# A four-layer hybrid decoder trunk: another order of issue on each engine, from four lists put together instead of one with a second merge

## The chip, the cores and the metric

The kernel runs on one core of a Trainium2 chip. The metric is the device time of one execution in microseconds (us): the median of three runs before the change was 2625.46 us (2624.12 to 2626.32).

## What is computed

Four layers, each `x = x + gate * mixer(rmsnorm(x) * (1 + scale) + shift)`, on 1024 positions of width 1024, batch 1, all in float32. Shift, scale and gate come from `c @ ada_w[i] + ada_b[i]`. Layers 0 and 3 mix with HGRN2, layer 1 with sliding-window attention, layer 2 with a gated DeltaNet. Each mixer has one input projection, a mixing part, a SiLU gate and one output projection. The change's prediction is mostly on layer 2:

```python
def gdn_mixer(h, w_in, w_out, conv_w, a_log, dt_bias, onorm_g):
    qkv, z, a, b = jnp.split(h @ w_in, [GD_QKV, GD_QKV + GD_VW, GD_QKV + GD_VW + GD_V_HEADS], axis=-1)
    qkv = jax.nn.silu(causal_conv(qkv, conv_w))
    q, k, v = jnp.split(qkv, [GD_QKW, 2 * GD_QKW], axis=-1)
    ...
    o = gated_delta_scan(q, k, v, beta, g)
    o = rmsnorm(o, onorm_g).reshape(B, T, GD_VW).astype(h.dtype)
    return (o * jax.nn.silu(z)) @ w_out
```

In the scan each chunk solves a triangular system `(A + I) X = rhs`, takes `v_new = u - w S`, gives an output from the old state and `v_new`, and updates the state: `S = S * exp(d_last) + k^T v_new`. The next chunk needs the new S.

## The kernel before, in words

**Tiles.** Activations are kept transposed (128 channels by 512 positions, two halves). A projection is split in three float32r matmuls per 128-row step, hi by hi, lo by hi and hi by lo (`mm3`, called with lines L350, L351, L352 for its three matmuls); a group of 8 steps, 24 matmuls of 128x512, fills one PSUM bank (`proj_ps`; other names for other projections: `projw_ps`, `projt_ps`, `outp_ps`, `out_ps`). Weights come by DMA from SyncE (`w_raw`, L319), ScalarE makes the hi part (`w_hi`, L321 or L324), VectorE the lo part (`w_lo`, L322 or L325).

**Layer 2 (`gdn`).** Its work is cut in eight units u of two value heads. Unit u runs its scan while unit u+1 has its triangular inverse made and later units are projected. The pieces that the prediction names:

- *Projections*: the evacuation of q, k and v is `conv`: ScalarE copies the bank to `gd_xs` (L820) and multiplies by the last tap into `gd_tb` (L824, after which the bank is free), VectorE adds three taps (L826), ScalarE takes a tanh (L832), VectorE multiplies (L833, into `gd_q`, `gd_k`); then TensorE transposes (`qtr_ps`, `ktr_ps`, `vtr_ps`, L839), ScalarE squares and sums (L846), and VectorE goes on from the sums (`gd_ms`, L880). The evacuation of z is a tanh on ScalarE and one product on VectorE (L918, after which the bank is free).
- *The inverse* (`inverse`): 31 pairs of VectorE instructions (L973, L974) fill `gd_Tb`; it goes through DRAM (L977 out, L983 back), ScalarE puts it in `gd_Tc` (L984), VectorE transposes that to `gd_Uc` (L986), and TensorE makes the rest in four rounds of small matmuls (`z_ps`, L1002 the first).
- *The scan* (`scan`), eight chunks a unit, each a chain from engine to engine: TensorE `ks_ps` (L1070, L1071, from the state and k, q); VectorE `gd_y` (L1076, for two heads); TensorE `w_ps` (L1081); ScalarE `gd_ws` (L1082); TensorE `S_ps` (L1086); VectorE `gd_S` (L1092), which the next chunk's `ks_ps` needs. Beside it ScalarE makes `gd_wg` (L1096) and TensorE the output (`w_ps`, L1097).

**What sets the order.** The program is first recorded by functions that weave such streams together. At its end `in_order` takes, for each engine, the recorded instructions and issues them in an order read from a table of numbers, `ORDER`: byte n of an engine's table means that the n-th instruction of those still left comes next (values from 255 up are spelled in three bytes). Each engine carries out its instructions in that order, and waits at one whose operands aren't there. Buffers, instructions and dependences are set before that, so the table moves instructions and nothing else, but for ScalarE's table loads, which are put in afterwards where its functions change.

```python
    for e, table in ORDER.items():
        left, places, last = rest[getattr(mybir.EngineType, e)], iter(zlib.decompress(base64.b85decode(table))), None
        for n in places:
            i = left.pop(n if n < 255 else next(places) + 256 * next(places))
            if last is not None:
                how = mybir.DependencyInfo(mybir.DependencyClass.NoSync, mybir.DependencyReason.DATA)
                tc.add_manual_dep(i, last, how, reason="order")
            last = i.name
```

Of the kernel before, what the change touches and what calls it, by code (L numbers as in the profile page):

```python
# [22 lines left out]
P = 128  # L23
T = 1024
D = 1024
# [31 lines left out]
        "iwx`sRaG)%n;9&`wg^-}vk$8Bfgq(0bLMh`yeg$%91-I{rUNP*(qh<haKcQxkV{%berc<`?^bC8mnktaaK)n6P-wjm0si<P%K!qk2Da%1?*4"
        "An?NWr!m2{}31KUZv=7zYm#0n7FkwWAJKJv<FU$*rR1Y$l&LkV(=fdH7&3R{-D?1%xkBgAe>EF{iV4cVksXahUemcK-DwyTEBfhHV|>b`*@h"
        "(v;AK47(7bq^Z2-|N-)iDKPJsYQoESY#w(6+4}`T+J!$L+1B)nMJTXniy^e24!WWepY@31A3StZI=YOPX^Q9V_^0$P(4b0^)G#ZEDhtQ2F_<"
        "cG=TpmAx$(I#m}#<uC}FZVC$letO2R2s1gZPXtdy2f<fwWt`WzVQp@badQg3y@7f$P=`;y-guJk)K>1Kutp?M$-Gq(~`{%lK>+t9r0A$p%`S"  # L60
        "-s9@MWRu3*lw@+(u9j@0qPsleHEZg&Sr=je={Q!-a4XNnf4%j&|X{h1^B_q@$(<Z@>MvIf;P1dtrWF{eFP1_<eW}?l}|OdmyJD@81uLu)r6$"
# [1733 lines left out]
```

## Time and profile before

| | |
|---|---|
| median of 3 runs | 2625.46 us |
| the profiled execution | 2630.06 us |
| its span, first to last instruction | 2628.4 us |
| TensorE busy in the span | 2542.7 us (97%) |
| VectorE, ScalarE busy | 2014.9 us (77%), 1328.7 us (51%) |
| mean granted TensorE clock | 0.988 of full |

The times of an instruction are from this one execution. A row of the timeline has the start, the duration, the engine and line, the operation, the output and inputs, the shapes, how many in a row, and in brackets how long the engine was idle before it and whose end it waited for. A row of the waits has a waiting instruction, the one that released it, the total in us, how often, and the longest. In a table of windows each engine has its busy us with the number of its instructions; PEclk is the clock granted to TensorE.

By time the span falls in a start (0 to about 60 us), layer 0 (to about 490), layer 1 (to about 1090), layer 2 (to about 1990) and layer 3.

### The profile page before, as it was taken

To read this page: it belongs to the slowest core of one execution; us is meant where nothing else is said; L and a number is where in the kernel's file an instruction comes from. 1 tells how busy PE (TensorE), PEld (TensorE's weight loads), DVE (VectorE), ACT (ScalarE), POOL (GpSimd) and SP (SyncE) were. 2 spreads that over 40 slices of the span, in tenths; PEclk is the share of its full clock that TensorE was granted. 3 is DMA by queue.
4 is the path that set the end of the run, shared out by engine and by line. 5 is a ranking of instruction groups with operands and counts; after the bars stand their busy time and mean duration, and the time that the engine had idled before them with its cause. 6 is when DMAs were issued, how large, how long until landed. Compare 5 with 4: busy or idle time off the path is not lost.

```text
span 2628.4 us, 50793 instructions
## 1 busy us (share of the span) xinstructions
PE 2542.7 (97%) x18271; PEld 2058.0 (78%) x18271; DVE 2014.9 (77%) x5663; ACT 1328.7 (51%) x3480; POOL 164.7 (6%) x382
## 2 busy tenths in 40 slices
PE   7999999999999999999999999999999999999999
PEld 4777887788988877787777788778788877788877
DVE  5585789886787868678889989888776846468775
ACT  4444344543465656455566666565644534344452
POOL 0001000001000000100011101100222000000000
PEclk8999999999999999999999999999999999999999
DMA  7333444644233343444344344333576412122443
GB/s 262 99 112 106 129 128 122 192 126 141 69 97 97 112 138 102 133 110 111 86 111 115 90 124 114 88 85 90 164 239 199 133 37 84 51 85 66 139 146 117
DMA packets 393618, 312.07 MB, mean 119 GB/s; under 512 B 74979, under 2 KB 320150, under 8 KB 393366
## 3 DMA queue, kind: packets, MB, share of 16 engines
q1 hardware_dynamic: 380822, 267.92, 34.5%
q0 software_dynamic: 12544, 40.90, 4.9%
q8 instruction: 144, 2.36, 0.4%
q14 instruction: 108, 0.88, 0.1%
HBM read 247.84 MB, written 60.88 MB: 117 GB/s over the span
## 4 chain that ended last, share of the span: by engine, by line
PE 80%; DVE 7%; DMA 6%; issue 4%; ACT 3%; SPq 0%; POOL 0%; DVEq 0%; ACTq 0%; POOLq 0%
PE proj_ps L350 12%; PE proj_ps L351 12%; PE proj_ps L352 12%; PE outp_ps L350 4%; PE outp_ps L351 4%; PE outp_ps L352 4%; PE projw_ps L352 2%; PE projw_ps L351 2%; PE projw_ps L350 2%; DMA ada_w<-in_ada_w_dram 2%; PE projt_ps L350 2%; PE projt_ps L351 2%; PE projt_ps L352 2%; PE lev_ps L1253 1%; PE pv_ps L1653 1%
## 5 line engine op out<-in xcount | busy, mean ns | idle before, releaser
L350 PE MATMUL proj_ps<-hhi,w_hi 128*128 128x512 f32 x1664 | 677.0, 407 | 16.4 <-ACT gd_tb L824 9.9
L352 PE MATMUL proj_ps<-hhi,w_lo 128*128 128x512 f32 x1664 | 673.4, 405 | 0.0
L351 PE MATMUL proj_ps<-hlo,w_hi 128*128 128x512 f32 x1664 | 672.1, 404 | 0.0
L350 PEld LDWEIGHTS proj_ps<-hhi,w_hi 128*128 128x128 f32 x1664 | 315.2, 190 | 80.2 <-ACT gd_tb L824 15.6
L352 PEld LDWEIGHTS proj_ps<-hhi,w_lo 128*128 128x128 f32 x1664 | 315.1, 189 | 58.2 <-issue 1.6
L351 PEld LDWEIGHTS proj_ps<-hlo,w_hi 128*128 128x128 f32 x1664 | 315.4, 190 | 56.7 <-issue 1.4
L321 ACT CAST w_hi<-w_raw 128x512 fp32r<-128x512 f32 x356 | 216.5, 612 | 266.2 <-PE proj_ps L351 150.9
L322 DVE TENSOR_TENSOR w_lo<-w_raw,w_hi 128x512 fp32r<-128x512 f32 x356 | 238.7, 675 | 129.6 <-ACT w_hi L321 124.0
L350 PE MATMUL outp_ps<-o_hi,w_hi 128*128 128x512 f32 x576 | 228.4, 398 | 1.6 <-ACT o_hi L1458 1.0
L351 PE MATMUL outp_ps<-o_lo,w_hi 128*128 128x512 f32 x576 | 229.5, 399 | 0.1
L352 PE MATMUL outp_ps<-o_hi,w_lo 128*128 128x512 f32 x576 | 228.8, 398 | 0.1
L324 ACT ACTIVATE w_hi<-w_raw,par 128x512 fp32r<-128x512 f32 (+1 forms) x136 | 94.5, 697 | 142.4 <-PE outp_ps L351 84.8
L826 DVE SCALAR_TENSOR_TENSOR gd_tb<-gd_xs,taps,gd_tb 128x512 f32<-128x512 f32 x192 | 146.0, 760 | 13.2 <-ACT gd_tb L824 12.4
L576 DVE SCALAR_TENSOR_TENSOR ada_acc<-ada_w,par,ada_acc 128x512 f32<-128x512 f32 x154 | 115.2, 748 | 35.1 <-DMA ada_w<-in_ada_w_dram 34.4
L350 PEld LDWEIGHTS outp_ps<-o_hi,w_hi 128*128 128x128 f32 x576 | 108.7, 189 | 25.0 <-issue 2.5
L325 DVE SCALAR_TENSOR_TENSOR w_lo<-w_raw,par,w_hi 128x512 fp32r<-128x512 f32 (+1 forms) x136 | 97.4, 718 | 39.9 <-ACT w_hi L324 39.5
L351 PEld LDWEIGHTS outp_ps<-o_lo,w_hi 128*128 128x128 f32 x576 | 108.9, 189 | 23.1 <-DVE o_lo L1459 1.5
L352 PEld LDWEIGHTS outp_ps<-o_hi,w_lo 128*128 128x128 f32 x576 | 108.9, 189 | 22.4 <-issue 0.9
L1450 POOL DMA_DIRECT2D o_in<-od x72 | 38.8, 539 | 1183.2 <-DVE sw_zs L1593 321.0
L350 PE MATMUL projw_ps<-w_hi,hhi 128*128 128x512 f32 x256 | 101.6, 402 | 2.4 <-DVE hg_q L1169 2.3
L351 PE MATMUL projw_ps<-w_lo,hhi 128*128 128x512 f32 x256 | 102.5, 402 | 0.0
L352 PE MATMUL projw_ps<-w_hi,hlo 128*128 128x512 f32 x256 | 102.4, 402 | 0.0
(431 smaller groups left out, 5386.3 us busy)
## 6 DMA issues: line engine op xcount, KB each, us to landing
ada_w<-in_ada_w_dram SPq DMA_DIRECT2D x160, 256.0 KB, 2.8
w_raw<-in_hg_in_w_dram SPq DMA_DIRECT2D x148, 256.0 KB, 2.9
w_raw<-in_gd_in_w_dram SPq DMA_DIRECT2D x128, 256.0 KB, 3.0
o_in<-od POOLq DMA_DIRECT2D x72, 256.0 KB, 3.6
x<-xd SPq DMA_DIRECT2D x64, 256.0 KB, 4.8
w_raw<-in_gd_out_w_dram SPq DMA_DIRECT2D x64, 256.0 KB, 3.2
xd<-x POOLq DMA_DIRECT2D x48, 256.0 KB, 2.7
w_raw<-in_sw_in_w_dram SPq DMA_DIRECT2D x44, 256.0 KB, 3.0
```

The source lines that it names most:

```text
L321: nc.scalar.copy(hi, raw)
L322: nc.vector.tensor_tensor(lo, raw, hi.bitcast(F32), ALU.subtract)
L324: nc.scalar.activation(hi, raw, AF.Copy, scale=scale)
L325: nc.vector.scalar_tensor_tensor(lo, raw, scale, hi.bitcast(F32), ALU.mult, ALU.subtract)
L350: mm(out, a[0], b[0], start=start, stop=False)
L351: mm(out, a[0], b[1], start=False, stop=False)
L352: mm(out, a[1], b[0], start=False, stop=stop)
L576: self.step = self.nc.vector.scalar_tensor_tensor(acc, w, c, acc, ALU.mult, ALU.add)
L826: last = nc.vector.scalar_tensor_tensor(y, xs[:, j:j + HT], w(j), y, ALU.mult, ALU.add)
L1253: return nc.tensor.matmul(pl[gs, n, c * 48:(c + 1) * 48], k[:, c * P + g * 32:c * P + (g + 1) * 32], x[:, 4 * c + g, :], start=True, stop= ...
L1450: nc.gpsimd.dma_start(t, od[(k0 + k) * P:(k0 + k + 1) * P, sl])
L1653: self.tied([lambda b=b, a=a: nc.tensor.matmul(po[a * 64:(a + 1) * 64], vg[:, n + 1 - nkb + b, :], p4s[b][:, :, a, :], start=b == nkb - 1, ...
```

## The change

`ORDER`'s five tables are replaced; no other line is touched. The new table is put together from four lists, one per layer, each made with assumed times of its own for handing a result from engine to engine, and TensorE's list isn't merged a second time afterwards. The tables tell a reader nothing; one line of TensorE's:

```diff
-        "c-rlo>2nmv6~N!FW>>qqZwawlohu2nI*?!`ap*z<gySF)?1(!7a~KHm2jU2m3J`<{kV>4wI1q4Ta8+W5xSVoTlFzB6Dqr#~Uy}SM`INk)dv>"
...
+        "c-rk+>u*%Y6+gSa`?Rr*4Xp7CWBj%kY}Q^dwy_Cs0>p%XAq7$zNT97Ms3L`wsDxlbfHZxC&_IE<snjM)TSaLiwe*p+A1YN<KU9_4Z~a?(9y9"
...
```

Every engine has the same instructions as before, except that ScalarE has 6 table loads instead of 8. Nearly all moves are short, within a layer. The new table text is two lines longer, so each line number after it is 2 higher in the changed kernel: L1083 there is L1081 here.

**TensorE at the end of a unit's scan.** In the first unit of layer 2, the seventh chunk and the first matmuls of the eighth. `ks_ps`, `w_ps` and `S_ps` are the scan's, `proj_ps` a projection's. Before:

```order
L1070 MATMUL ks_ps_14825<-gd_S_14741,gd_k_12988 128x256
L1071 MATMUL ks_ps_14825<-gd_S_14741,gd_q_13049 128x256
L1081 MATMUL w_ps_14824<-gd_y_14843,gd_uq_13096 128x128 x2
L1086 MATMUL S_ps_14861<-gd_ws_14850,gd_kt_13030 128x256
L1097 MATMUL w_ps_14824<-gd_wg_14849,gd_uq_13096 128x128 x2
L1070 MATMUL ks_ps_14946<-gd_S_14863,gd_k_12988 128x256
L1071 MATMUL ks_ps_14946<-gd_S_14863,gd_q_13049 128x256
L350 MATMUL proj_ps_14813<-hhi_11748,w_hi_14802 128x512
```

The same chunk in the changed kernel, from its first `w_ps` to its `S_ps`:

```order
L1083 MATMUL w_ps_14824<-gd_y_14843,gd_uq_13096 128x128
L353 MATMUL proj_ps_14679<-hlo_12498,w_hi_14597 128x512
L354 MATMUL proj_ps_14679<-hhi_12497,w_lo_14598 128x512
L352 MATMUL proj_ps_14679<-hhi_12497,w_hi_14597 128x512
L353 MATMUL proj_ps_14679<-hlo_12498,w_hi_14597 128x512
L354 MATMUL proj_ps_14679<-hhi_12497,w_lo_14598 128x512
L1083 MATMUL w_ps_14824<-gd_y_14843,gd_uq_13096 128x128
L352 MATMUL proj_ps_14679<-hhi_12497,w_hi_14597 128x512
L353 MATMUL proj_ps_14679<-hlo_12498,w_hi_14597 128x512
L354 MATMUL proj_ps_14679<-hhi_12497,w_lo_14598 128x512
L1088 MATMUL S_ps_14861<-gd_ws_14850,gd_kt_13030 128x256
```

The chain stood bare, one scan matmul behind the other; now three to five projection matmuls stand between a scan matmul and the one that needs its result. The projection group `proj_ps_14679` stood ahead of these chunks before.

**VectorE at the start of layer 2's first inverse rounds.** `gd_q` is the conv's end, which TensorE's transposes wait for, L918 frees a projection's bank, `ada_acc` is a step of layer 3's modulation that waits for a DMA. Before:

```order
L322 TENSOR_TENSOR w_lo_14298<-w_raw_14296,w_hi_14297 128x512
L826 SCALAR_TENSOR_TENSOR gd_tb_13982<-gd_xs_13980,taps_472,gd_tb_13982 128x512
L576 SCALAR_TENSOR_TENSOR ada_acc_14060<-ada_w_14352,par_102,ada_acc_14060 128x512
L833 SCALAR_TENSOR_TENSOR gd_q_13979<-gd_tb_13983,gd_tb_13982 128x512
L322 TENSOR_TENSOR w_lo_14304<-w_raw_14302,w_hi_14303 128x512
L880 TENSOR_SCALAR gd_ms_13647<-gd_ms_13647 128x16
L298 TENSOR_SCALAR rs_y_14002<-gd_ms_13647 128x16
L918 SCALAR_TENSOR_TENSOR gd_tb_14123<-gd_tb_14123,proj_ps_14052 128x512
```

In the changed kernel:

```order
L324 TENSOR_TENSOR w_lo_14298<-w_raw_14296,w_hi_14297 128x512
L828 SCALAR_TENSOR_TENSOR gd_tb_13982<-gd_xs_13980,taps_472,gd_tb_13982 128x512
L835 SCALAR_TENSOR_TENSOR gd_q_13979<-gd_tb_13983,gd_tb_13982 128x512
L988 STREAM_TRANSPOSE gd_Uc_13629<-gd_Tc_13619 128x512
L947 TENSOR_TENSOR gd_tmp_14093<-gd_tmp_14093,gd_cmask_12433 128x512
L1006 COPY gd_Z_12445<-z_ps_13682 32x16x32
L882 TENSOR_SCALAR gd_ms_13647<-gd_ms_13647 128x16
L920 SCALAR_TENSOR_TENSOR gd_tb_14123<-gd_tb_14123,proj_ps_14052 128x512
```

The `ada_acc` step and the second `w_lo` no longer stand ahead of `gd_q` and L918, and the transpose of `gd_Tc` and the evacuation of the first `z_ps` round now stand ahead of L918.

**TensorE at the same place.** Before, the transposes are followed by a projection:

```order
L352 MATMUL proj_ps_14139<-hhi_12497,w_lo_14135 128x512
L839 MATMUL qtr_ps_13991<-ident_86,gd_q_13979 128x128 x4
L350 MATMUL proj_ps_14216<-hhi_11748,w_hi_14205 128x512
L351 MATMUL proj_ps_14216<-hlo_11749,w_hi_14205 128x512
L352 MATMUL proj_ps_14216<-hhi_11748,w_lo_14206 128x512
```

In the changed kernel they are followed by the first round of the inverse:

```order
L354 MATMUL proj_ps_14139<-hhi_12497,w_lo_14135 128x512
L841 MATMUL qtr_ps_13991<-ident_86,gd_q_13979 128x128 x4
L1004 MATMUL z_ps_13681<-gd_Tc_13619,gd_uq_13096 32x32
L1004 MATMUL z_ps_13682<-gd_Tc_13619,gd_uq_13096 32x32
L1004 MATMUL z_ps_13681<-gd_Tc_13619,gd_uq_13096 32x32
```

The round needs `gd_Tc`; eleven matmuls of `proj_ps_14216` stood ahead of it before and none does now.

More of the change, by code (lines that the diff above doesn't have):

```diff
@@ L57 @@
[L57 to L61, printed above, removed]
@@ new lines @@
+        "mOoxQtv7u;5;{Ykrb?!7Z}XU;iu=A1JJAPf<LzH#_}csr~iY}&MDW@d(q6AZUe60xBMk<Zs7mLSYN(@WC?dR3pUqbG3}Qe)}TrLd$A;U5fFh"
+        "#{~XjoL%)Gx0$PxY9=!q$%~))%8;gU0q$U3OZpWbifK|hc;-17HEd$(9{GOSOz#^XoLp;m|lg8@Csaj`KG3(D@~<Iea3(LMOX-ohCtU_Z(-3"
+        "Qe7I~`7eI5f)EKfLPuC*oI!S*s{Ah3x+$Z5+mZwtq*U(T_gW(W(HODOkbhg%lJlz2oL!jGVwqW<a0zuc8EM)m@-XmH7jw6iQL<0Zn>xCmn)x"
+        "#5o%_fELhvAPQD5S+_7GP=$pKsgdR{6w&*Z7|yC>ZA7EST^9VxhP&d<|ZLbLY5-1^tZia=0j+m-etQP?EeDfEJG|g4IRp^73l7pGFxD7x=#7"
+        "F?4i1>?~L-*IOE!mA~V}^_I{c0<2Y4C8Li-ar;<eA;Bu#K+1yb69~H2@*UEZTQykJV(`v^SC@2UQj1VFT}n|4k;&L^69}0C4t;qDB1p1$JW7"
@@ new lines @@
+        "<SLS5)b#3Lv`wFU1fU3o)ow1-k{lgrz1%OqPg1V+^=3*{^xSKi}c!sR$MWMUvYYHS+T1aZfM$Pt2V48FrXxkg%Lf|jCC>j6YdgsZ&eR$8o<7"
+        "3vvnC(+=L*vaIg5JX7;aW*k`5)lj5hXWSBlM*?OK?FOA32hRlDEVc|QAD(QDTOd%2|=0|tqA*lO-&<$i?y}2Kr>frB+831T4D(PehA>LEf(n"
+        "?hX9I*$G0s6&+Y3L;6IO;1}b2jKduv(+J0zWkl>KKRMjD3wF-*vOuQ($0!fzHaP}8tM`Pnd&TBMgW0j3qXDkRoOC=DMk7|tp*Ml()N4m85l!"
+        "8wO1nAiX1onPR07nT6Drof!0B@aoXl>P6Ay8aB*n=qSjNRBfNe$Ls-!HDJP9WTy=U-G$&LG}Igc3xY0<>h$&Ck!9FZRNoJ+NEfZP@~F6W)d!"
+        "@RnKWt#{zy&4X~@O?ZlK-*_DX@H7H%;5uA`0|>Ll`|#d-@DnNjtWEF%{?zL`Kk%x4hj8!SJvczUKM63a-#mrT<=qH?ci_7`K2P<zrEj<%(<^"
@@ new lines @@
+        "+ra2|n<)ZD$fyK{H$%o&4w5~0hx5M0o1*ZUVPTp&N|-FM-KZi`uX0x6~G^zp|unh!suGLho-9f*0jbm`L7t5*ZbfA8L|yLWfNPIUYXJcfWjA"
+        "+Wp=af)!7|4;dvQ@ic34Zg(SF@Kfej(#g_fz6w#G>!1QQzF9om+^Py$`#!ka!S*6?_R##g*)&)xXtC0CqX3b%ZMAdZrwszK=8Zg5QWm=hmZ3"
+        "g3FiS$qtL>0aPltE^!DxBUqRfwDYbaI$k&^t1lY&<w`Hhs<C|WEtCueypFe)-_|@Yio3?v<7!lB`OA~iZ5TA_&;SyN0>mkA0m-5gSD?=N%K|"
+        "@8;7!Uyc41nI=-fT82#tl@l37bsr*dfc+RTbt|qx(61`gH0PB*n2G7#JWsrKhI{Mn*=&2^vfdr23V?cLSl#DuBE|`Wa&Y<Z?L?uFv4pPvLhy"
+        "XA_MX&ysOp>}Svdnw>pz<VYbsegl#F5%?uqe4iL5oM*~usYAItdGh4hvuAa~-y*o6gJcSAo|55>y|M9m2K9mh%};*~_wU26C?*B#AP-}@HqI"
@@ new lines @@
+        "{x@MnY@k2<A+@>(!>tULn4;Bn52S}Be^!=R1MP~U5j0WfUFwg4HNoipHlV*)k+2bK;2Y(QXXPH_ZAWdy1{T}5IlK~)-}$`mo9sPQ<(?no|BO"
+        "vL7<3vN{LI7$&ZjI<VJU>cN3256wk#>Q7P&}wkoQ`=*PoFQ~y*#kl^s>9wB-I@~SG&fLl=Oh_RfxBH6?2^weP)xG`NCaG{C`>p9Z8){GkXeQ"
+        "o^cZ_1vF>hdsgZTMa^=cy26Pc*`0efb+D^gVLF5<o4GmFDamb4=+opolM#&ncXiwG^vf$c=Q9?0eKP>}o8bw%SVNFrOvXLvMYMJDs5DRJ^h("
+        "n0MD-Qz<^kmX+994#LIoo5Ql;SqwhL2L>%Y>pJOrS_rpJ`Ivq{+=LbJDmLon)$BQBy4H(gX?W56W<z?Exh%1h*|eI3}27oG|dh=MiT-yby@O"
+        "cWm*T7Z+D-ItrUpt&0~g8JK6h#-O(gtul;gzlTm)v_l1lU{$d=WJE#I607H<3MZaQLzTlzh_+QGEBk^R_J~Au@FNlj9qvqf2Wg2#Zd8#>0*V"
@@ new lines @@
+        "ldG)EjLpIRy2J_7Sg{ike2QkrWP{a0nHzC>D9*;%KxAy7%DGMR*hGKS+Ff&+<9TnSRbpTArp-PBLj@XY049pq0sElfG3q*E_>WRab88ZDjp7"
+        "?yPU`w$dMI<>7x^WBduEVOhTM8F}KgM)N8N2zCrK%%1i_LbQOS$d9dss8VHVE+QQv6QX"),
+    "Activation": (
+        "c-oCtiE`sM3<WQVI<5O~?AXp`cW2uE|M&F)pd6>2=@fP>h9bd-hl41JK)KJnC$c2cG!4~T*s?sP$rHsG3;Ypn83oemuCu2kWLnG^Yl-#Xy~}"
+        "c<U<{^I0$J8nP;?H@ECeD)j)nOB=Ju1LZL_Ni)qUBO*x+1S;9S~y-%384vTPXmbe4U`<RJ{cQX8zza~-*8a%xD<Hil?&BazW}jFmDxC+sjC9"
+        "by_)1pK-l5|5X<esm=2()vc9#>}vNpzp$*7!h5SWvsrG$&K9dTo}@i>+x*OQ$T-121G?m6B&=GmULU65U@gcAkRey-LUCamJE9b;w1^Y&dGw"
+        "JV7Imy)!1597W)NW4pbf=XY65KBj%NSL>a{yl)UWJrr1+A;Fy!pR%5M@?>J02XqqNtp&*Z<;1l?z1V#XC$0K;G_nk**ga8kF1f0+FVKA3V#)"
+        "h$m^BL<fZ~?(nxE$grSl$w1gn1@-&wN9z)dQFkRSHKKBjI)}%Qtx`mO1ebhF*e^>Kb<Sec~Qatom-kJE4Bt(w=?yILYC}eFtN?0O13ImB_}i"
+        ")_cpIi`4hTo+qK?q(K$q4~YH)pA`Gv^Jz?XNreWCI}%gf!z$XA*_)=ayj%`DZiW<JU6UPWpiQZOcSXtt#&m?OXsS3ZrfJ9A@@w^CBWvNfs2k"
+        "36rcK<9Szt1z#1Z-EhqYQXmgW?^5O!})n@$Wde#A#zM=2a>(WprmYHGZul{~<<wIB9TviE$bg39Gme(LD`5A|TX5Ig-!qV@62Sg{TS1m@DP1"
+        "u*{&<IUJ)I#;j?N&ZPcLS3IaM1Ldc(@fKpP2)(*J>}vwZTlK%o@X_1ngadQ?7vZ{BrqP?!Q+;7gd#W$z88IqRzc>uwh0^uC3F8~Ik6C5Nb&@"
+        "UeNeQg_R%7Zl08e)Ofz5+GGUmPAM<=Bg|ai2c~M|M7RK=xJ)xCKhQ9?J^pM%JBBj5cl}>mGzhzm5;$YBNPG@`>YAl)<>k86QhdR;s?{s~Z13"
+        "=40@HGrSfh0i#lnrzL6WVBC7+0hj)bzz%93cc~Sr$=2kPQ+}RaO=i%9X?rFlIU5GN=r>t$?tz6V=GkX|Bd`UGI0I3qC3{I7G6BCwc3>ZQDv`"
+        "&liUjTXn0sh3bB9>HXbz5>(ggco~BR=kN|eLGt`moI~hIB9)w8Y#elpl#3(Mlslv<xO>lN91{qRCSh;>T)y1O+%4;JrUdL6aj2T@_1@lYw}C"
+        "!BKKx@9ss>sGn?OR<+^&!V8)X7bFE9lsk$gatQq!KOxi{UvB5n*EaX@ybBly=ftTZb!KuvDt8@|0VvfIE_j5a|uhK;^KdtvPrnizpXsQJkmW"
+        "w~9TG|130a7-TU1L`_J7j@G%eP46JLE~?P<|l7QJsihm$%Wn||Fn@o8Iy}kD<0oLxDD{&=EI^g8?K~((Vt9}jOp>9J74l-&a#P_GyTytAVZ%"
+        "0Luw3iE~V1YxHN}TQNdfjWn-b0Hnmb%0&q%!l^VgbC?zfh5|HBCKtq%}px`?rNcp8!>Wm8RAtfvrulGu7x$0-n<pGDQ3%#^lQeTa>T){19+v"
+        "Y>4E?*liw{gP-hq3bRkbg8>&B4O6;X>^&Ii;ILBH3xLWWHJ;KTAjSz2Tygj`d`9eMlRQ^<OPiT5mWWrJ>XHM}ziX`d2huNq?3Uy1~h!10y;i"
+        "Zn&hQ;!?#87d77-E_U!s!*#}rT^la0iz-_7_4?*o=7SG`Ua#{n`5UImNwN"),
@@ new lines @@
+    "SP": (
+        "c-o~@=}yBi40h67O_z0pu0w;3a*Rs|@s|fd976E^Z-MQkEiFSJ;U9_P<CD(-{6tbp5CU)HFCT_FWsukiFRe8wB$K?zkJzG!7J%xgV>$ZzL?m"
+        "=zEf_Ol-a!FF9jYRWx`B%PEF?2vOyVgnZTq)lWqq(Z+BDub{)CN4dSuqera3*oxZ;$A5b!HySvInKe1d0qf!DWp_!t?B9o)zwQU6Z&;aY5(Q"
+        "`DTCZT}S5091w`vrH*XHCKwGmd;J5D-`Iuu9aK#tt>h|P|v6Vd0Cc=#R68H)x2J6<*ItKVIMj)E6UjE0)up|ah}hSmdoMD_<TyY_Z7E*@;1>"
+        "^h_d7|P|MJh^c>Vqln6qnB_}IAkDTRKMiYUv5<$XmD836Nx0YaRM#bVodhU<beOi<k%-XjLfl<0*<P0PwxywX|fqpQKXn-<p`L8InQ7saIKt"
+        "hQAeLg9QE|OFfA})-<R6?i$DpDMz8JTyZ=eTWJnb^Ki&iCWG@f(AHw0?f#Lg{9E)mQm{h<223%zONIL`64Iy!re^;E%win~-cI!O{ILiG?m8"
+        "elR4d=r{1|W8ZXt%-Qzx+T7gU-T$<%R1dLpk6YO%Ge8(G"),
```

149 lines of the change are left out of this document (56 added, 93 removed).

## The prediction

> **What bounds the kernel now.** First the page's head: the span and what each engine did of it.
>
> ```profile
> span 2628.4 us, 50793 instructions
> PE 2542.7 (97%) x18271; PEld 2058.0 (78%) x18271; DVE 2014.9 (77%) x5663; ACT 1328.7 (51%) x3480; POOL 164.7 (6%) x382
> ```
>
> TensorE (PE) is the bound. No instruction is added or taken from it, so the change can only give back what isn't useful work: about 2628.4 - 2542.7 = 85.7 us of idleness, and matmuls that run at a lowered clock. Next the windows, one per layer, to see where that lies.
>
> ```profile
> 0.00:60.00 60.00, 44.96 (x159) 25.34 (x160) 35.41 (x110) 25.09 (x44) 1.11 (x8) 0.82 0.79 287
> 60.00:490.00 430.00, 419.66 (x3728) 335.33 (x3727) 320.69 (x1032) 186.08 (x475) 11.01 (x45) 1.00 0.41 123
> 490.00:1090.00 600.00, 589.86 (x3753) 490.21 (x3753) 477.59 (x1239) 319.35 (x747) 35.77 (x74) 0.99 0.37 115
> 1090.00:1990.00 900.00, 858.16 (x5774) 698.48 (x5773) 755.92 (x2055) 526.06 (x1588) 95.84 (x216) 0.99 0.43 120
> 1990.00:2629.00 639.00, 630.03 (x4862) 508.68 (x4860) 425.24 (x1231) 272.12 (x630) 20.95 (x39) 1.00 0.33 102
> ```
>
> TensorE is idle for 15.0 us in the start, 10.3 in layer 0, 10.1 in layer 1, 41.8 in layer 2 and 9.0 in layer 3. Half of it is in layer 2, where VectorE works 755.92 of 900 us as well. So third, TensorE's waits in layer 2.
>
> ```profile
> PE proj_ps L350 <- ACT gd_tb L824: 9.9, 10, 1.6
> PE proj_ps L350 <- DVE gd_tb L918: 4.8, 2, 2.4
> PE w_ps L1081 <- DVE gd_y L1076: 3.9, 5, 0.9
> PE S_ps L1086 <- ACT gd_ws L1082: 3.0, 6, 0.6
> PE w_ps L1097 <- ACT gd_wg L1096: 2.6, 6, 0.6
> PE w_ps L1081 <- ACT gd_ws L1082: 2.5, 5, 0.5
> PE ks_ps L1070 <- DVE gd_S L1092: 2.3, 3, 1.2
> PE qtr_ps L839 <- DVE gd_q L833: 1.5, 1, 1.5
> ```
>
> Five of the rows are links of one chain, the scan: 3.9 + 3.0 + 2.6 + 2.5 + 2.3 = 14.3 us in 25 waits. They aren't spread over the 64 chunks. They stand in clusters where TensorE has run out of projection matmuls to put between the links, as the timeline of one unit's end shows.
>
> ```profile
> 1277.48 0.40 PE L352 MATMUL proj_ps<-hhi,w_lo 128*128 128x512 f32 x1
> 1277.71 0.39 PE L350 MATMUL proj_ps<-hhi,w_hi 128*128 128x512 f32 x1
> 1277.94 0.38 PE L1081 MATMUL w_ps<-gd_y,gd_uq 128*128 128x128 f32 x2
> 1278.08 0.48 PE L351 MATMUL proj_ps<-hlo,w_hi 128*128 128x512 f32 x1
> 1278.39 0.40 PE L352 MATMUL proj_ps<-hhi,w_lo 128*128 128x512 f32 x1
> 1278.78 0.70 PE L1086 MATMUL S_ps<-gd_ws,gd_kt 128*128 128x256 f32 x2
> ...
> 1281.06 0.59 PE L1071 MATMUL ks_ps<-gd_S,gd_q 128*128 128x256 f32 x2
> 1282.58 0.49 PE L1081 MATMUL w_ps<-gd_y,gd_uq 128*128 128x128 f32 x2 [0.92 <-DVE gd_y L1076]
> 1283.53 0.49 PE L1081 MATMUL w_ps<-gd_y,gd_uq 128*128 128x128 f32 x2 [0.46 <-ACT gd_ws L1082]
> 1284.47 1.22 PE L1086 MATMUL S_ps<-gd_ws,gd_kt 128*128 128x256 f32 x2 [0.46 <-ACT gd_ws L1082]
> ...
> 1289.36 0.63 PE L351 MATMUL proj_ps<-hlo,w_hi 128*128 128x512 f32 x1
> ```
>
> A link over ScalarE takes 0.84 us from start to start when ScalarE is free (1277.94 to 1278.78, with two projection matmuls between), and as much or more with nothing between (0.94 from 1283.53 to 1284.47): the matmuls between cost no time, and without them TensorE stands.
>
> **The change, part by part.** *The scan's links.* I counted in the two orders how much TensorE work stands between a matmul whose result is handed out and the one that waits for it, over the five kinds of link above: 30 of 274 links have at most one 128x512 matmul between in the order before, 5 of 274 in the new one. Most others now have three or more. A matmul pair of the scan lasts 0.14 us to the next start (1277.94 to 1278.08) and a projection matmul 0.23 (1277.48 to 1277.71), so three of them and the pair make at least 0.14 + 3 x 0.23 = 0.83 us, the 0.84 of a free ScalarE link. So 25 of 30 bare links get cover, and I let the same share of their waits go: 25/30 x 14.3 = 11.9 us saved. What is late next at these places is the projection, whose matmuls now go between the links instead of ahead of them: its bank must be free about a group later, which is harmless while L824 and L918 keep their places.
>
> *The clock behind the bare links.* The windows around three such clusters have the granted clock in the column ahead of the DMA share.
>
> ```profile
> 1285.00:1290.00 5.00, 4.48 (x13) 3.48 (x12) 4.11 (x13) 3.41 (x16) 0.00 (x0) 0.50 0.22 56
> 1290.00:1295.00 5.00, 5.00 (x23) 4.16 (x23) 3.02 (x10) 1.96 (x6) 0.10 (x1) 0.87 0.01 2
> 1660.00:1665.00 5.00, 5.00 (x18) 4.08 (x18) 3.90 (x15) 2.72 (x14) 0.00 (x0) 0.66 0.20 52
> 1880.00:1885.00 5.00, 4.14 (x15) 3.44 (x16) 1.98 (x5) 2.19 (x8) 1.06 (x2) 0.68 0.18 67
> 1890.00:1895.00 5.00, 5.00 (x23) 4.17 (x21) 3.25 (x7) 2.63 (x9) 2.32 (x5) 0.80 0.58 193
> ```
>
> Busy time times the missing share of the clock is what a dip costs: 4.48 x 0.50 + 5.00 x 0.13 + 5.00 x 0.34 = 4.6 us for the first two clusters, 4.14 x 0.32 + 5.00 x 0.20 = 2.3 for the third. In the new order the first two clusters are covered throughout; the third, in the last unit, keeps some of the bare links, so I take half of it: 4.6 + 1.2, say 6 us saved.
>
> [...]
>
> *Links that get shorter.* To cover the bare links the new order spreads the same matmuls over more places: nine links over `gd_y` have about three matmuls between, and none of that kind had in the old order. VectorE can be busy when such a link asks for it: with nothing between the link took 1.52 us from start to start (1281.06 to 1282.58). With the pair's own time and three matmuls about 1.1 us of it is covered. Bounds: 0 to 0.4 us for each of nine, 0 to 4 us; I take the middle, 2 us lost.
>
> *VectorE's order at 1217 us.* Two steps move out of the way of `gd_q` and of L918.
>
> ```profile
> 1216.28 0.74 DVE L826 SCALAR_TENSOR_TENSOR gd_tb<-gd_xs,taps,gd_tb 128x512 f32<-128x512 f32 x1
> 1217.92 0.75 DVE L576 SCALAR_TENSOR_TENSOR ada_acc<-ada_w,par,ada_acc 128x512 f32<-128x512 f32 x1 [0.90 <-DMA ada_w<-in_ada_w_dram]
> 1218.59 0.68 DVE L833 SCALAR_TENSOR_TENSOR gd_q<-gd_tb 128x512 f32<-128x512 f32 x1
> ```
>
> The step that waits for its DMA for 0.90 us goes behind `gd_q`, which can start 1.6 us sooner (1218.59 against 1216.28 + 0.74). But TensorE meets the inverse's first round next, and that needs `gd_Tc`.
>
> ```profile
> 1212.65 0.18 DVE L974 TENSOR_TENSOR gd_Tb<-gd_Tb,gd_tmp 128x16 f32<-128x16 f32 x1
> ...
> 1222.62 0.67 ACT L984 COPY gd_Tc<-gd_tmp 128x512 f32<-128x512 f32 x1 [0.48 <-DMA gd_tmp<-tblk]
> ```
>
> From the last L974 to the end of L984 are 1223.29 - 1212.83 = 10.5 us through DRAM. In the new order three VectorE steps of about 0.7 us (a `w_lo`, the other half's `gd_q`, an `ada_acc`) stand behind the last L974 instead of ahead of it, so `gd_Tc` may come 1 to 3 us earlier, still after the transposes. The 1.5 us wait for `gd_q` and most of the 2.4 us wait for L918 become one wait for `gd_Tc` of about the same length. Between a gain of 3 and a loss of 3 I take 0.
>
> *Everything else.* The largest wait of layer 2, 9.9 us for L824, keeps about a whole group of 24 matmuls between in both orders: 0, at most half of it gained or as much lost. The start (15.0 us) has the same DMA order and nearly the same TensorE order: 0. Layers 0, 1 and 3 have 10.3, 10.1 and 9.0 us of idleness, in short single waits; there the links change both ways: 0, between 5 gained and 5 lost. The two table loads that go were on ScalarE, which is idle half the time: 0 to 2 us gained, taken as 0.
>
> The sum is 11.9 + 6 - 2 = 15.9, say 16 us less. Against the profiled execution, 2630.06 us (its span and 1.7 us around it), that is 2614.1. That execution lies 4.6 us above the median of the runs, so the forecast for a median is 2625.5 - 16 = **2609.5 us**.
>
> **The rivals.**
>
> *No gain.* A projection matmul covers one link only. Those now put into the bare clusters are gone from where they stood, and the projections run later against the scan, so their banks may be asked for sooner than L824 frees them: about 30 groups in the layer losing half a microsecond each is 15 us, and all is given back. For it speaks that L824's wait is the largest already, and that VectorE works 84% of the layer. Against it, the count of bare links falls without many others getting under three matmuls. Time: **2625.5**.
>
> *Slower: the inverse's round waits for `gd_Tc`.* TensorE's first `z_ps` round stands right behind the transposes, with nothing between, in the unit shown; in four of the eight units 0.5 to 1.1 us less work stands ahead of it than before, by my count of the orders. If VectorE doesn't end the L973/L974 run earlier, TensorE stands until the trip of 10.5 us is over, and L918, now behind the transpose of `gd_Tc`, keeps the projection's bank too. At 2 us a unit, 8 x 2 = 16, the gain is gone; at 3.1 us a unit the kernel is 25 us above the forecast: **2634.5**. Against it, the three VectorE steps above stand behind the run now. No row shows what L973 and L974 do in the new mix.
>
> *More.* The list for layer 2 may relieve L824, L918 and `gd_q` too: half of 9.9 + 4.8 + 1.5 is 8 us, and half of layer 0's idleness 5 more: **2596.5**. Only the one place at 1217 us speaks for it.
>
> [...]
>
> **How the numbers follow.** Forecast 0.50, no gain 0.18, slower 0.14, more 0.10, the clock stays 0.08. The likeliest gives 2609.5. Its own range, with the bounds above (2 either way for the short links, 3 at 1217 us, 5 for L824, 5 for the other layers, not all on one side), is 2600 to 2618. The range that should hold 8 in 10 reaches from the better rival to past no gain, 2594 to 2630, and leaves out the slower one. A measurement of this kernel can tell about 0.2%, 5.3 us, from no change. Faster by more than that are the forecast, more and the clock: 0.50 + 0.10 + 0.08 = 0.68; within it no gain, 0.18; slower 0.14.
>
> **What would show it.** In the changed profile the five scan rows of TensorE's waits in layer 2 should sum to 3 to 5 us instead of 14.3, TensorE's idleness from 1090 to 1990 us should fall from 41.8 to about 30, and the windows behind the first and fifth units' scan ends should have a clock near 1.00. The waits for L824 should stay near 10 us. The prediction is wrong if the scan rows fall but other rows of that view rise by as much (then the first rival; the slower one if they are `z_ps` on `gd_Tc`), or if the span's idleness moves into another layer.

## The result and the profile after

The changed kernel took 2607.2 us (median of 4 runs, 2605.29 to 2609.54), the kernel before 2625.89 beside it (4 runs, 2624.12 to 2626.53): 18.7 us less by the medians. The ratio of the two kernels, which the later runs are compared by, is 0.9917 with a 95% interval of 0.9900 to 0.9933, which would be 21.8 us (17.6 to 26.3). Its profiled execution took 2606.59 us, with a span of 2604.9. Line numbers are 2 higher now.

The page's head, and the windows of layer 0 and layer 2 (columns as before: PE, PEld, DVE, ACT, POOL busy, clock, DMA share, GB/s):

```profile
span 2604.9 us, 50803 instructions
PE 2535.7 (97%) x18271; PEld 2054.6 (79%) x18271; DVE 2015.9 (77%) x5663; ACT 1325.8 (51%) x3478; POOL 159.4 (6%) x382
```

```profile
60.00:490.00 430.00, 421.99 (x3768) 337.19 (x3767) 322.06 (x1036) 185.54 (x477) 12.11 (x48) 1.00 0.41 124
1090.00:1990.00 900.00, 872.11 (x5858) 708.38 (x5858) 767.65 (x2076) 535.10 (x1599) 97.19 (x228) 0.99 0.46 125
```

The span is 23.5 us shorter. TensorE's idleness falls from 85.7 to 2604.9 - 2535.7 = 69.2 us, by 16.5, and its busy time by 7.0 us, for the same instructions. In the window of layer 2 it is 900 - 872.11 = 27.9 instead of 41.8 us. But layer 2 begins and ends earlier now: the same TensorE work lies between 1086 and 1968 us, where TensorE is busy for 852.25 of 882 us, so 29.8 us idle, 12.0 less than before, and about 30 was forecast. In layer 0 the idleness is 8.0 instead of 10.3. TensorE's waits from 1086 to 1968 us:

```profile
PE z_ps L1021 <- DVE gd_uq L1016: 3.7, 5, 1.1
PE w_ps L1083 <- DVE gd_y L1078: 3.5, 4, 1.5
PE proj_ps L352 <- ACT gd_tb L826: 3.3, 4, 1.3
PE z_ps L1004 <- ACT gd_Tc L986: 3.0, 3, 1.5
PE proj_ps L352 <- DVE gd_tb L920: 1.9, 1, 1.9
...
PE w_ps L1099 <- ACT gd_wg L1098: 1.3, 2, 0.8
...
PE S_ps L1088 <- ACT gd_ws L1084: 1.1, 2, 0.5
...
PE w_ps L1083 <- ACT gd_ws L1084: 0.4, 1, 0.4
...
PE ks_ps L1072 <- DVE gd_S L1094: 0.3, 2, 0.2
```

The five scan rows sum to 3.5 + 1.3 + 1.1 + 0.4 + 0.3 = 6.6 us instead of 14.3, where 3 to 5 were forecast. The wait for a projection's bank (L826, L824 before) fell from 9.9 to 3.3, where it was forecast to stay near 10, and the wait for `gd_Tc` rose from 0.6 to 3.0 us. The end of the first unit's scan, bare before, on the timeline:

```profile
1274.01 0.38 PE L1083 MATMUL w_ps<-gd_y,gd_uq 128*128 128x128 f32 x2
1274.14 0.48 PE L353 MATMUL proj_ps<-hlo,w_hi 128*128 128x512 f32 x1
...
1275.38 0.38 PE L1083 MATMUL w_ps<-gd_y,gd_uq 128*128 128x128 f32 x2
...
1276.30 0.62 PE L1088 MATMUL S_ps<-gd_ws,gd_kt 128*128 128x256 f32 x2
```

The same three matmuls stood at 1282.58, 1283.53 and 1284.47 before, with 0.92, 0.46 and 0.46 us of idleness ahead of them; now there is none, and the clock is 1.00 from 1270 to 1290 us. But the place at 1217 us has a dip of the clock that is longer than before. First its waits on the timeline, then the windows:

```profile
1215.18 0.66 PE L841 MATMUL qtr_ps<-ident,gd_q 128*128 128x128 f32 x4 [0.73 <-DVE gd_q L835]
1217.35 1.20 PE L1004 MATMUL z_ps<-gd_Tc,gd_uq 32*32 32x32 f32 x64 [1.51 <-ACT gd_Tc L986]
1219.49 0.18 PE L1012 MATMUL z_ps<-gd_Uc,gd_Z 32*32 32x32 f32 x1 [0.94 <-DVE gd_Z L1006]
```

```profile
1215.00:1220.00 5.00, 2.37 (x117) 2.05 (x119) 2.70 (x6) 4.04 (x15) 2.46 (x4) 1.00 0.92 253
1220.00:1225.00 5.00, 5.00 (x100) 4.00 (x93) 4.91 (x12) 2.82 (x8) 1.63 (x3) 0.51 0.31 112
1225.00:1230.00 5.00, 5.00 (x36) 3.65 (x34) 2.96 (x13) 1.20 (x2) 0.00 (x0) 0.50 0.35 105
```

Busy time times the missing share of the clock is 5.00 x 0.49 + 5.00 x 0.50 = 5.0 us here. Summed like this over the 5-us windows from 60 us on, the clock costs 14.6 us in this profile and 16.1 in that of before; in layer 2 alone 8.4 and 10.5.

### The profile page after: what moved, and what is told of

The parts are those of the page before. It is cut to its first block, busy times and chain, and to the rows that moved or that the text cites. A ratio compares the mean times of both kernels' runs of the same rounds, so it can differ in the third digit from the quotient of the medians.

```text
span 2604.9 us, 50803 instructions
## 1 busy us (share of the span) xinstructions
PE 2535.7 (97%) x18271; PEld 2054.6 (79%) x18271; DVE 2015.9 (77%) x5663; ACT 1325.8 (51%) x3478; POOL 159.4 (6%) x382
## 4 chain that ended last, share of the span: by engine, by line
PE 76%; DVE 9%; DMA 7%; issue 4%; ACT 2%; SPq 1%; POOL 0%; DVEq 0%; POOLq 0%; ACTq 0%
PE proj_ps L352 11%; PE proj_ps L353 11%; PE proj_ps L354 11%; PE outp_ps L352 4%; PE outp_ps L353 4%; PE outp_ps L354 4%; PE projw_ps L353 2%; PE projw_ps L354 2%; PE projw_ps L352 2%; DMA ada_w<-in_ada_w_dram 2%; PE projt_ps L353 2%; PE projt_ps L354 2%; PE projt_ps L352 2%; PE lev_ps L1255 1%; DVE gd_tb L828 1%
## 5 line engine op out<-in xcount | busy, mean ns | idle before, releaser
L828 DVE SCALAR_TENSOR_TENSOR gd_tb<-gd_xs,taps,gd_tb 128x512 f32<-128x512 f32 x192 | 145.7, 759 | 11.9 <-ACT gd_tb L826 8.8
```

The source lines that it names most:

```text
L828: last = nc.vector.scalar_tensor_tensor(y, xs[:, j:j + HT], w(j), y, ALU.mult, ALU.add)
```

## The experiments

Where two orders are joined, they are cut at places at which both had issued the same instructions on each engine. All comparisons are with the kernel before on the same chip.

**Layer 2's list alone.**

```diff
 start, layers 0 and 1: the order before
-layer 2: the order before
+layer 2: the changed kernel's order
 layer 3: the order before
```

> The new order in layer 2 alone; the start and layers 0, 1 and 3 keep the order before. Theory (the gain is layer 2's: scan links with cover, projection banks freed sooner, clock behind the scans' ends): by the times of the same instructions in the two profiles layer 2 gives 18.7 of the 23.5 us, so 17 to 19 us below the kernel before, a ratio near 0.993. The prediction's own sum put 16 us there. Rival (the gain is spread over the four lists, or the layers help each other): less than 10 us, a ratio over 0.996.

Measured: 0.9945 (0.9929 to 0.9961), 14.4 us less. The five scan rows sum to 6.5 us, the wait for L826 is 3.3 and that for `gd_Tc` 3.0, the same as in the changed kernel to 0.2 us. So most of the gain is layer 2's. The 14.4 us (10.2 to 18.7 by the interval) lie below the 17 to 19 of the theory, which the interval doesn't exclude, and above the rival's 10.

**The other lists alone.**

```diff
-start, layers 0 and 1: the order before
+start, layers 0 and 1: the changed kernel's order
 layer 2: the order before
-layer 3: the order before
+layer 3: the changed kernel's order
```

> The new order in the start and layers 0, 1 and 3; layer 2 keeps the order before. Theory: the delays of the two profiles give 2.1 us in the start and layer 0, 1.5 in layer 1 and 1.7 in layer 3, so 4 to 6 us below the kernel before, a ratio near 0.998, and layer 2's waits as before (five scan rows near 14 us). The prediction had 0 for these layers, between 5 gained and 5 lost. Rival (spread gain): 10 us or more.

Measured: 0.9982 (0.9973 to 0.9992), 4.7 us less. The waits in layer 2 are those of before (9.9 for L826; the scan rows 3.7 + 3.0 + 2.5 + 2.4 + 2.0). The two parts make 14.4 + 4.7 = 19.1 us. The whole, by its ratio as well, gave 21.8, and 20.5 and 22.6 us in its two repetitions below. With intervals of about 4 us either way the parts add up to the whole; that the lists help or hinder each other isn't seen.

**Cover taken away again.** In the changed kernel the projection matmuls in the links at seven units' scan ends go ahead of them. For the first unit:

```diff
+L354 MATMUL proj_ps_14679<-hhi_12497,w_lo_14598 128x512
 L1083 MATMUL w_ps_14824<-gd_y_14843,gd_uq_13096 128x128
-L353 MATMUL proj_ps_14679<-hlo_12498,w_hi_14597 128x512
...
 L1083 MATMUL w_ps_14824<-gd_y_14843,gd_uq_13096 128x128
-L352 MATMUL proj_ps_14679<-hhi_12497,w_hi_14597 128x512
...
 L1088 MATMUL S_ps_14861<-gd_ws_14850,gd_kt_13030 128x256
```

> The changed kernel with the links at seven units' scan ends laid bare again: TensorE's projection matmuls that stand in the seventh chunk's links (in units 1, 2, 5 and 6 also in the last links of the sixth) go ahead of these links in one piece; nothing else moves. Theory (cover is worth the idleness and the clock): a bare end stood idle for 0.61 + 0.92 + 0.46 + 0.46 + 0.52 = 3.0 us in the profile before and cost 2.9 us of clock. Four long ends and three of one chunk: 16 to 20 us of idleness and 11 us or more of clock, 25 to 32 us slower than the changed kernel, with windows under 0.90 of the clock behind at least the four long ends. [...] Rival (covering links is worth nothing, the time comes from elsewhere): under 5 us.

Measured: 1.0045 (1.0031 to 1.0060) of the kernel before, where the changed kernel has 0.9917: 0.0128 x 2626 = 34 us slower than the changed kernel, slower even than the kernel before. TensorE's waits in layer 2, the scan rows first, and five windows at or behind bare ends (the first unit's, and those of units 1, 3, 5 and 6):

```profile
PE w_ps L1083 <- ACT gd_ws L1084: 5.1, 5, 3.1
PE w_ps L1083 <- DVE gd_y L1078: 4.9, 8, 1.1
PE S_ps L1088 <- ACT gd_ws L1084: 4.3, 9, 0.5
PE w_ps L1099 <- ACT gd_wg L1098: 4.2, 8, 0.8
...
PE proj_ps L352 <- ACT gd_tb L826: 3.3, 4, 1.4
...
PE ks_ps L1072 <- DVE gd_S L1094: 2.0, 4, 0.9
```

```profile
1280.00:1285.00 5.00, 5.00 (x25) 4.00 (x23) 5.00 (x16) 4.31 (x18) 0.11 (x1) 1.00 0.40 110
...
1370.00:1375.00 5.00, 3.79 (x12) 3.12 (x13) 3.34 (x12) 3.01 (x13) 0.00 (x0) 0.67 0.39 106
...
1565.00:1570.00 5.00, 2.45 (x6) 1.68 (x6) 3.46 (x9) 3.13 (x12) 0.00 (x0) 0.62 0.03 3
...
1755.00:1760.00 5.00, 3.97 (x14) 3.12 (x15) 3.30 (x13) 3.71 (x15) 0.00 (x0) 0.74 0.31 87
...
1845.00:1850.00 5.00, 3.89 (x11) 3.05 (x12) 3.10 (x12) 1.85 (x8) 0.00 (x0) 0.61 0.15 54
```

The scan rows sum to 20.5 us, 13.9 more than in the changed kernel. Over the whole span (2636.8 us, TensorE busy for 2548.0) the idleness is 88.8 us, 19.6 more than in the changed kernel, and the busy time 12.3 us more: together the 31.9 us by which the spans differ. Of the 12.3 us, the windows put 20.9 - 14.6 = 6.3 down to the clock; the other 6 are taken up below. Three of the four long bare ends have a dip behind them, where the theory had all four: behind unit 2's the clock stays at 1.00. Of the three ends that are bare for one chunk, the first unit's and unit 4's leave it at 1.00 too; unit 3's has a dip, with a single wait of 3.08 us for a `gd_ws` that ScalarE makes late, behind work on transposes. The clock's 6.3 us are fewer than the 11 of the theory, and the loss is a little above its 25 to 32 us, with 6 us of busy time that it hadn't counted. The runs say the same of the clock: its mean over ten of them is 0.9867, against 0.990 for the changed kernel. So cover is worth both idleness and clock, as the theory had it, and the rival doesn't hold. The wait for L826 stayed at 3.3 us: it does not hang on this cover.

**The place at 1217 us put back.** TensorE has projection matmuls ahead of the first round again, VectorE the step that frees their bank ahead of the transpose, ScalarE its half ahead of `gd_Tc`. VectorE's part:

```diff
 L835 SCALAR_TENSOR_TENSOR gd_q_13979<-gd_tb_13983,gd_tb_13982 128x512
+L882 TENSOR_SCALAR gd_ms_13647<-gd_ms_13647 128x16
+L920 SCALAR_TENSOR_TENSOR gd_tb_14123<-gd_tb_14123,proj_ps_14052 128x512
 L988 STREAM_TRANSPOSE gd_Uc_13629<-gd_Tc_13619 128x512
 L947 TENSOR_TENSOR gd_tmp_14093<-gd_tmp_14093,gd_cmask_12433 128x512
 L1006 COPY gd_Z_12445<-z_ps_13682 32x16x32
-L882 TENSOR_SCALAR gd_ms_13647<-gd_ms_13647 128x16
-L920 SCALAR_TENSOR_TENSOR gd_tb_14123<-gd_tb_14123,proj_ps_14052 128x512
```

> The changed kernel with one place put back as it was before: at 1215 us VectorE and ScalarE again do the two evacuations of z ahead of the first inverse's gd_Tc and gd_Uc, and TensorE again has 11 projection matmuls ahead of the first z_ps round and 6 behind it (17 fewer at later places of the same unit). Theory (the new dip of the clock at 1220 to 1230 us comes from the stretch of idleness and 32x32 matmuls behind each other): idleness at the place stays within 1 us, the dip shrinks from 5 us to the 1 to 2 us it cost before, 3 to 4 us faster than the changed kernel, about 2603.5. Rival (the dip hangs on the idleness alone, which stays): no change, within 1 us.

Measured: 0.9910 (0.9894 to 0.9926), which can't be told from the changed kernel's 0.9917; nor can the 3 to 4 us of the theory be told from nothing at these intervals. The waits at the place and the windows:

```profile
1215.42 0.66 PE L841 MATMUL qtr_ps<-ident,gd_q 128*128 128x128 f32 x4 [0.74 <-DVE gd_q L835]
1218.52 0.50 PE L352 MATMUL proj_ps<-hhi,w_hi 128*128 128x512 f32 x1 [2.44 <-DVE gd_tb L920]
```

```profile
1220.00:1225.00 5.00, 5.00 (x169) 3.88 (x170) 2.12 (x4) 2.37 (x6) 2.89 (x5) 1.00 0.44 160
1225.00:1230.00 5.00, 5.00 (x78) 3.78 (x69) 4.54 (x14) 3.06 (x7) 0.00 (x0) 1.00 0.27 70
```

The idleness is the same 3.2 us, in two waits instead of three with small matmuls between, and in this profile the dip is gone: 5 us of clock are back. A second profile of the same kernel, from the comparison on one chip below, has a dip there again, a shorter one:

```profile
1215.00:1220.00 5.00, 2.56 (x7) 1.99 (x7) 3.05 (x6) 2.67 (x11) 2.02 (x3) 0.68 0.79 225
1220.00:1225.00 5.00, 5.00 (x75) 3.78 (x74) 0.73 (x2) 0.78 (x2) 1.98 (x4) 0.64 0.31 112
```

That is 2.56 x 0.32 + 5.00 x 0.36 = 2.6 us, against 5.2, 6.3 and 6.0 us around this place in the three profiles of the changed kernel. So the dip gets smaller, and doesn't reliably go. Layer 2's idleness, over the same TensorE work, is 32.4 us instead of 29.8, and in the later pair of profiles 30.3 instead of 28.4. The matmuls that went to this place are missing at later ones: two waits of the first unit that the changed kernel hasn't, 0.84 us for L920 and 0.96 us for `gd_k`, are the largest there. So some 2 us of the gain at one place were given back at others.

**Two attempts to keep that gain.** The first adds cover at the `z_ps` rounds that wait (3.7 us in the changed kernel), in units 1, 2, 3 and 5; the second leaves this out, mends the two waits in the first unit, and runs beside the place alone and the changed kernel.

```diff
 unit 5, ahead of the third round:
-7 matmuls of proj_ps, then L1021 z_ps_19982
+11 matmuls of proj_ps, then L1021 z_ps_19982
```

> The kernel with the place at 1215 us put back, and cover at six more waits: in units 1, 2, 3 and 5 one to four projection matmuls more ahead of the inverse's third round (L1021, which waited 0.84, 0.41, 0.58 and 0.99 us), two ahead of unit 5's first round (L1004, 0.40 us), taken from longer runs behind; in unit 0 three more ahead of the transposes that waited 0.96 us. Theory (a matmul between costs nothing where TensorE stands): 3 to 4 us less than with the place alone, so 4 to 8 us below the changed kernel, ratio to the kernel before about 0.989 to 0.990. Rival (the projections so moved ask for their banks sooner and wait there): no gain over the place alone.

> The changed kernel once more, beside the kernel before on this chip, so that the two kernels below have it as their neighbour: 0.990 to 0.993 of the time before. In the first five runs of experiments the times of one kernel lay up to 0.6% apart and went with the mean clock of the run (on the kernel before, 21 runs, about 1.7 us for each 0.001 of the mean clock). If that holds, this kernel's runs spread in the same way, and its mean clock is about 0.001 above that of the kernel before.

Measured with the added cover: 0.9937 (0.9925 to 0.9949), and the changed kernel on the same chip 0.9922 (0.9908 to 0.9936). It is not faster than the changed kernel, and the 3 to 4 us over the place alone, which ran on another chip, aren't seen. TensorE's waits:

```profile
PE proj_ps L352 <- ACT gd_tb L826: 7.9, 8, 2.0
PE proj_ps L352 <- DVE gd_tb L920: 5.1, 3, 2.4
...
PE z_ps L1021 <- DVE gd_uq L1016: 1.5, 2, 1.1
```

The waits of the `z_ps` round fell from 3.9 us (with the place alone) to 1.5, and those for L826 rose from 3.5 to 7.9. This is the prediction's first rival, at a place where it decides: projections that run ahead of their evacuations wait for their bank.

```diff
 ScalarE, ahead of gd_sq_14116 (L1107):
+L919 ACTIVATE gd_tb_14292<-proj_ps_14216 128x512
 VectorE, ahead of gd_tmp_14266 (L947):
+L920 SCALAR_TENSOR_TENSOR gd_tb_14292<-gd_tb_14292,proj_ps_14216 128x512
```

> The place at 1215 us put back as before, without the cover at the z_ps rounds that made the projection banks late, and with two waits mended that the first version of this had in unit 0: three projection matmuls more ahead of the transposes that waited 0.96 us, and the evacuation that freed a bank 0.84 us late (L919 on ScalarE, L920 on VectorE) moved to where both engines stood idle, 4 to 6 us earlier. Theory: 1.8 us less than the place alone, idleness of TensorE in layer 2 near 30 us, no window under 0.90 of the clock at 1215 to 1230 us, mean clock near 0.993 in most runs: 3 to 5 us below the changed kernel. Rival (the clock's dips only move elsewhere, the idleness is what counts): the same as the changed kernel.

> The place alone once more, on the chip of the mended version and of the changed kernel: theory 1 to 3 us below the changed kernel at a mean clock 0.002 to 0.003 higher; rival: the same.

> The changed kernel on the same chip as these two: 0.991 to 0.993 of the kernel before, mean clock 0.989 to 0.991, windows near 0.50 of the clock at 1215 to 1230 us.

Measured on one chip: mended 0.9926 (0.9910 to 0.9941), the place alone 0.9923 (0.9908 to 0.9937), the changed kernel 0.9914 (0.9897 to 0.9930). All three are the same within their intervals. Mean clocks over their runs were 0.9910, 0.9914 and 0.9898. The two waits, 1.8 us, are gone in the mended version, but its row for L826 is 5.0 us where the place alone has 3.5, and its clock still drops at the place, to 0.75 and 0.56 in the windows from 1210 to 1220 us. So neither the gains that were expected of these two versions nor a clock that stays up were measured. No version here beats the changed kernel.

**The clock by itself.**

```diff
+    def links(n, name):
+        for k in range(n):
+            t = ps.tile([P, P], F32, name=name, tag="link", bufs=2)
+            nc.tensor.matmul(t, lk[0], ident, start=True, stop=True)
+            nc.scalar.copy(lk[0], t)
...
+        for n, name in ((1, "la"), (2, "lb"), (4, "lc"), (8, "ld"), (16, "le")):
+            dense(90)
+            links(n, name)
```

> A kernel that computes nothing of the reference (its output is a piece of x, repeated). TensorE alternates 90 dense 128x512 matmuls (about 20 us) with one of fifteen disturbances, five times each: 1, 2, 4, 8 or 16 bare links over ScalarE (about 0.46 us of idleness in each 0.94 us); one single wait of about 1.5, 2.7, 4, 6 or 9 us; 64, 192 or 448 matmuls of 32x32 without a wait; and the place at 1215 us of the changed kernel (wait, transposes, 1.5 us wait, 64 small, wait, 48 small), with the same place with one longer wait and no small matmuls. Theory (the clock follows how much of the last few us the array worked, in whatever pieces): one or two links leave it alone, 8 and 16 lower it to 0.50 in most of the five turns; waits of 2.7 us do in some turns, by where they fall; 192 and 448 small matmuls do as well. [...]

The 90 dense matmuls last 20.66 us undisturbed; what they last longer behind a disturbance is what the lowered clock cost them. On the timeline, behind one link (`la`), behind a single wait of 1.32 us (`sa`), and two of the rows of eight links (`ld`):

```profile
27.98 0.49 PE L66 MATMUL la<-ident,lk 128*128 128x128 f32 x2 [0.35 <-ACT lk L64]
28.23 20.66 PE L57 MATMUL dense<-b,a 128*128 128x512 f32 x90
```

```profile
167.09 0.49 PE L75 MATMUL sa<-ident,big 128*128 128x128 f32 x2 [1.32 <-ACT big L73]
167.33 20.68 PE L57 MATMUL dense<-b,a 128*128 128x512 f32 x90
```

```profile
538.06 0.49 PE L63 MATMUL ld<-ident,lk 128*128 128x128 f32 x2 [0.35 <-ACT lk L64]
538.90 0.80 PE L63 MATMUL ld<-ident,lk 128*128 128x128 f32 x2 [0.35 <-ACT lk L64]
```

In the middle of the eight links the same matmul goes from 0.49 to 0.80 us, with no wait over 0.41 us anywhere. Over the five turns of each disturbance, in one run of this kernel:

| disturbance | dense matmuls behind it, us |
|---|---|
| 1 or 2 links, waits of 0.35 to 0.41 us | 20.66 to 20.70, all turns |
| 4 links | 22.04, 21.95, 20.68, 20.68, 20.68 |
| 8 links | 22.50 to 23.12, all turns |
| 16 links | 21.82 to 22.30, all turns |
| one wait of 1.32 us | 20.68, all turns |
| one wait of 2.68 us | 21.84 to 22.17, all turns |
| one wait of 3.98 us | 22.27 to 22.30, all turns |
| one wait of 5.92 us | 23.21 to 23.41, all turns |
| one wait of 9.17 us | 22.11 to 22.18, all turns |
| 64 matmuls of 32x32 | 20.69, all turns |
| the place of the changed kernel | 22.60 to 23.33, all turns |
| the same waits, no small matmuls | 22.26 to 22.29, all turns |

The theory holds for the links; the wait of 2.68 us cost something in every turn, where it had some of them. Waits of 0.41 us at most, eight in a row, lower the clock in every turn (22.50 to 23.12 us against 20.66), and so does a single one of 2.68 us (21.84 to 22.17); a single one of 1.32 us doesn't (20.68). That the clock follows how much of the last few us the array worked stays the author's estimate: the rows show what each disturbance cost, not what the clock goes by.

Where a disturbance falls counts as well: the same four links cost 1.38 and 1.29 us in two turns and 0.02 us in three. In the records of the granted clock of the two kernels' profiles, before and after, every low stretch but the last, which the end of the run cuts off, lasts one to four times 3.41 us, and all begin whole multiples of 3.41 us apart. On this kernel's timeline nine rows of links have a matmul of 0.49 us followed by one of 0.79 or 0.80, and these places lie whole multiples of it apart too, to within 0.5 us. Cut into these steps, the two turns in which four links lowered the clock had 3.33 and 3.06 us of one step filled by them, the other three 2.64 us at most. The five waits of 2.68 us all ended within about 0.4 us of a step's end, so what such a wait costs at another place isn't shown.

What 192 and 448 small matmuls cost is left out, since TensorE had waits of up to 1.7 us among them that the profile gives no cause for.

## Why the prediction was right, and where its sum was not

The time came out 2.3 us from the forecast, and the first term's mechanism is what the runs show. But the sizes were not the forecast ones: what the scan's waits and the clock gave less, the banks, the other layers and a price left out gave more. That the sum came so near is luck: several terms were off by 4 to 7 us each, and the errors cancelled.

- **The scan's links**, forecast 11.9 us saved: 14.3 - 6.6 = 7.7 us. The mechanism was right, as the bare ends show from the other side. What failed was letting the same share of the waits go as of the bare links. Of the 6.6 us that stay, some 4 lie in the last unit (1852 to 1897 us), where the prediction left bare links in the clock's term but not in this one, and 1.5 is one wait at 1433 us for a `gd_y` that VectorE makes late, whatever TensorE has between.
- **A price the sum left out.** A bare link costs more than the wait that its row shows. The `w_ps` pair at 1283.53 us before was busy for 0.49 us with nothing behind it, so its link took 0.94 us: 0.46 of idleness and 0.48 of a matmul that runs out alone. Covered, the pair at 1274.01 us takes 0.13 us to the next start. The rows of waits show the 0.46 only. In the sum of the spans this is busy time that goes: 7.0 us less busy, of which the clock's windows explain 16.1 - 14.6 = 1.5. The other 5.5 us are about what 25 links at up to 0.35 us each (0.48 - 0.13) can give, and the 6 us left over in the kernel with bare ends agree. That these are the same thing is worked out from rows, not tried by itself.
- **Everything else, L824** taken as 0 with at most half of 9.9 gained: 6.6 us gained. The step that failed looked only at how many matmuls stand between a group and the next one in its bank. It didn't look at when ScalarE frees the bank. Over 62 such banks the time from the last matmul to the end of L824 falls from about 6.5 to 5.2 us on average in the two traces, because L824 starts 4.74 us behind the end of L820 before and 3.21 now. Taken alone this wasn't tried: the engines' lists of layer 2 depend on each other.
- **The clock behind bare links**, forecast 6 us: the dips at 1285, 1660 and 1880 us are gone in this profile, as forecast. Only for the first is this sure: it shows in both profiles with the old list for layer 2 and in none of the changed order. The one at 1660 shows in only one of the two with the old list, and the last unit has a dip again in the two other profiles of the changed order, where the prediction let half of it stay. In their place stands the one at 1220 us, 5 to 6 us in the three profiles of this order, against 1.2 and 2.6 in the two with the old list for layer 2. The mean clock of the runs rose from 0.9889 (21 runs of the kernel before, 0.9889 again in 11 others) to 0.9903, 0.9897 and 0.9898 (4, 6 and 5 runs) only. At 1.7 us for each 0.001 (below) that is 1.4 to 2.4 us. That the dips have another cause than the bare links, the clock that stays, with its chance of 0.08, is refuted by the bare ends (6.3 us more of clock) and by the links of the last kernel (22.50 to 23.12 us behind eight, 20.66 undisturbed); with none of the 6 us gained it was nearer in this term all the same.
- **Links that get shorter**, 2 us lost: the row for `gd_y` went from 3.9 to 3.5 us, so nothing, or little.
- **VectorE's order at 1217 us**, 0: in idleness 3.97 us became 0.73 + 1.51 + 0.94 = 3.18, right to 0.8 us, one wait for `gd_Tc` taking the place of the others. That small matmuls stand between these waits now, and what this does to the clock, was not weighed.
- **The slower rival's wait** for `gd_Tc` is real: 3.0 us instead of 0.6, so 2.4 us more over the eight units where 25 were needed. It is in three units, not in all.
- **The other layers**, 0 with 5 either way: 4.7 us gained (2.1 to 7.1) when they ran alone, at the upper end of the bounds.

Together, in layer 2's idleness over the same work: 7.7 + 6.6 + 2.9 for L918 (4.8 to 1.9) + 0.8 for `gd_q` (1.5 to 0.7) = 18.0 us are given, and 2.4 for `gd_Tc` and 3.6 in smaller rows taken, such as `vtr_ps` (0.2 to 1.8) and `kk_ps` (none to 1.1); 41.8 - 29.8 = 12.0 us remain.

## What to carry to other kernels

Matmuls that are free to move were worth most here between the links of a chain from engine to engine: seven scan ends laid bare cost 19.6 us of idleness, by estimate 6 us of matmuls that run out alone, and 6.3 us more of clock by the windows, with a dip a few us behind four of the seven. Count, for each buffer that is waited for, when the engine that frees it gets to it (L824 began 1.5 us sooner behind L820, and the wait for it fell from 9.9 to 3.3 us), not only how much work stands before it is asked for. Cover was a fixed stock: matmuls put into one hole were missing in another (new waits of 0.84 and 0.96 us in the first unit), and groups brought forward waited for their banks (3.5 us became 7.9), so a local mend is judged by the whole layer's idleness.
